# Hybrid stick-breaking / RG-LRU block: sums of output-weight blocks made in DRAM, output projection with plain loads into rotating buffers

## The chip, the core and the metric

The kernel runs on one core of a Trainium2 chip. The metric is the device time of one execution in microseconds, median of several runs. A trace of one profiled execution lists every instruction of the engines: PE (matrix multiply; PEld its weight loads), DVE (vector), ACT (scalar), POOL (GpSimd) and SP, which here only issues transfers (DMA). ACT and POOL issue transfers too, between their own instructions. All transfers run on the core's 16 DMA engines.

## The reference

```python
xn = rmsnorm(h, norm_gain[l])                       # h: (1, 512, 2048)
proj = jnp.einsum('bsd,de->bse', xn, w_in[l])       # 2048 -> 6144
q, k, v, g_sb, x_lru, g_lru = jnp.split(proj, ...)  # 1024 each
y_sb  = stick_breaking_attention(qh, kh, vh) * silu(g_sb)    # 8 heads x 128
y_lru = rg_lru(causal_depthwise_conv(x_lru)) * silu(g_lru)   # 1024 channels, 8 groups
y = jnp.concatenate([y_sb, y_lru], axis=-1)
h = h + jnp.einsum('bse,ed->bsd', y, w_out[l])      # 2048 -> 2048
```

All is float32. The kernel multiplies a float32 matrix as a high half (cast to a shorter format) and a low half (the rest), so each product takes three matmuls: high x high, high x low, low x high.

## The kernel before

**Input projection.** Four rounds p = 0 to 3, one for two heads and two LRU groups each. A round has three groups of eight chunks: `qk` (queries and keys), `xg` (LRU input and its gate), `vg` (values and attention gate). A chunk is 256 rows of w_in, loaded by SP in two transfers of 256 KB into one of four raw buffers (L214 to L221, L239), split by ACT (high, L231) and DVE (low, L232), and used in 24 matmuls. Attention weights and the LRU of a round run beside the next groups. Finished rows of y go to `y_dram`; those of the last heads and LRU groups (6, 7, 14, 15) stay in SBUF. `finish_vg` (L479) ends a round: it evacuates the values and multiplies the attention weights with them (PE L416 and L418, tile `o`).

**Output projection.** It is a Strassen-Winograd scheme: y is cut into four blocks (`a11` to `a22`, tokens by channels), w_out into 2 x 2 blocks, and seven products `p1, p7, p5, p3, p6, p2, p4` (in this order) of combinations of them give the result. Products 1, 3 and 2 use plain blocks of w_out; 7, 5, 6 and 4 use sums of blocks. A product has 2 x 4 weight tiles (m, a), each 128 x 2 x 512 (512 KB), and for each of them a pair of casts (L581 on ACT for the high half `wo`, L582 on DVE for the low half) and 12 matmuls (L627 to L629). The combinations of y (`s1`, `s3`, `s5`, `s6`, `s7`; split into `s` and `os`) are made on DVE, and so are the sums of the results with the residual x (`r`, loaded from ACT's queue, L647) before the stores (SP, L652).

**How the weight tiles come.** c1 (8 tiles) and the first half of c2 (4 tiles) are loaded by SP (L550) into slots that lie over the input projection's buffers; the second half of c2 goes into memory that attention frees (`c2_pool`, L665). A sum is made in SBUF: POOL issues a second transfer of another block onto the same tile with `accum_op=add` (L554). For c1 that happens after each split of product 1, 5 and so on (`add_to`, L659, called through `after` in `product`, L621), so c1 runs through the blocks of products 1, 5, 6, 4. c2 is loaded and added to for product 7, and reloaded (`reload`, L689) for products 3 and 2. The high and low halves rotate through two buffers `wo0`, `wo1`, and from product 7 on a third (L593).

**What sets the order.** Within an engine the instructions stand in an order that the framework's scheduler chooses from its own estimate of times; `tc.issue_after(x)` makes what follows stand behind x. At most eight transfers of SP and ACT together are under way on their eight lanes: each issue waits until the transfer that last used its lane has landed. An engine's instructions are started strictly in order, so an issue that waits holds up what stands behind it.

Of the kernel before, what the change touches and what calls it, by code (L numbers as in the profile page):

```python
# [1 line left out]

# [6 lines left out]
F32 = mybir.dt.float32  # L9
F32R = mybir.dt.float32r  # L10
# [3 lines left out]
ALU = mybir.AluOpType  # L14
# [7 lines left out]
def hybrid_block_kernel(ctx: ExitStack, tc: tile.TileContext, x, norm_gain, w_in, q_norm_gain,  # L22
                        k_norm_gain, conv_w, conv_b, lru_w_a, lru_b_a, lru_w_x, lru_b_x,
                        lru_lambda, w_out, out):
    nc = tc.nc
    P = 128
# [4 lines left out]
    KC = 2  # L31
# [3 lines left out]
    x2 = x[0]  # L35
# [178 lines left out]
    def load_w(src, name):  # L214
        t = raw_pool.tile([P, KC, 512], F32, tag="raw", name=name)
        if len(src.shape) == 4:
            for s in range(2):
                nc.sync.dma_start(t[:, :, 256 * s:256 * s + 256], src[:, :, s, :])
        else:
            nc.sync.dma_start(t, src)  # L220
        return t  # L221

# [12 lines left out]
    def in_group(a, p, vfirst, name, first=False):  # L235
# [13 lines left out]
        for c in range(NC):  # L249
# [13 lines left out]
            for b in range(4):  # L263
                for j in range(KC):
# [15 lines left out]
                    else:  # L280
# [217 lines left out]
    for p in range(4):  # L498
# [7 lines left out]
        banks = in_group(2, p, False, f"xg{p}")  # L506
# [23 lines left out]
    proj.close()  # L530
    NA = 4
# [4 lines left out]
    for tag, cols in ([(f"yl{a}", 1024) for a in (3, 2, 1, 0)] + [(f"c2_0_{a}", 1024) for a in (3, 2, 1, 0)]
                      + [("wo1", 2048), ("s3", 1024), ("s2", 1024)]
                      + [(f"c1_1_{a}", 1024) for a in (3, 2, 1, 0)]
                      + [("wo0", 2048), ("s1", 1024), ("s0", 1024)]
                      + [(f"{n}{a}", 1024) for a in (3, 2, 1, 0) for n in ("c1_0_", "ye")]):  # L540
# [23 lines left out]
    c1 = {(m, a): two(f"c1_{m}_{a}") for m in range(2) for a in range(NA)}  # L564
    c2 = {(0, a): two(f"c2_0_{a}") for a in range(NA)}
    a11, a21 = [t[:, :, 0:256] for t in ye], [t[:, :, 256:512] for t in ye]
    a12, a22 = [t[:, :, 0:256] for t in yl], [t[:, :, 256:512] for t in yl]

    for a in range(NA):
        nc.sync.dma_start(ye[a], y_dram_a[0, :, a])  # L570
        load_c(c1[0, a], 0, 0, 0, a)
    for a in range(NA):
        load_c(c1[1, a], 0, 0, 1, a)
    for a in range(NA):
        load_c(c2[0, a], 0, 1, 0, a)
        add_c(c2[0, a], 1, 1, 0, a)

    def split(t, src):
        t = t.rearrange("p (x b n) -> p x b n", x=2, b=2)
        h, l = t[:, 0], t[:, 1]  # L580
        nc.scalar.copy(h, src)  # L581
        nc.vector.tensor_tensor(out=l, in0=src, in1=h.bitcast(F32), op=ALU.subtract)  # L582
        return h, l

    def split_s(i, a, src):
# [4 lines left out]
    def split_w_out(i, m, a, src):  # L590
        n = wo_count[0] % wo_count[1]
        wo_count[0] += 1
        if n == 2:  # L593
            return split(wo_pool.tile([P, 2048], F32R, tag="wo", name=f"wo{i}_{m}{a}"), src)
        return split(held.pop(f"wo{n}") if f"wo{n}" in held else op_tile(f"wo{n}", F32R, f"wo{i}_{m}{a}"), src)
# [4 lines left out]

    finish_vg(3, banks, wts)
    for a in range(2):
# [4 lines left out]

    def product(i, banks, src, w, after=None):


        out = {}
        s = []
        for m in range(2):
            for u in range(2):
                out[m, u] = banks(m, f"p{i}_{m}{u}")
            for a in range(NA):
                if m == 0:
                    s.append(ready.pop(("s", a)) if i == 1 else split_s(i, a, src[a]))
# [39 lines left out]

    def add_to(tiles, s, h):  # L659
        return lambda m, a: add_c(tiles[m, a], s, h, m, a)  # L660

    p1 = product(1, banks_1, a11, c1, add_to(c1, 0, 1))

    mixer.close()
    c2_pool = ctx.enter_context(tc.tile_pool(name="c2", bufs=4, reuse_waits="tile"))  # L665
# [22 lines left out]

    def reload(tiles, s, h):  # L689
        return lambda m, a: load_c(tiles[m, a], s, h, m, a)  # L690

    p7 = product(7, banks_mm, s7, c2, reload(c2, 1, 1))
    for a in range(NA):
# [75 lines left out]
```

## Time and profile before

| | us |
|---|---|
| median of 3 runs | 813.45 |
| lowest, highest | 812.19, 813.66 |
| the profiled execution, its own time | 810.3 |
| its span in the trace | 808.6 |
| PE busy | 774.3 (96%) |
| DVE, ACT busy | 512.5 (63%), 441.2 (55%) |
| share of the chain that ended last: PE, DMA | 90%, 5% |

PE is busy in nearly all of the span; of the page's 40 slices the 31st to the 34th (about 606 to 687 us) show less, 7, 7, 8 and 4 tenths, where DMA stands at nine tenths or more. How to read the rows below: a row of the timeline begins with the start and the duration of what it merges (x2 means two instructions), and in brackets stands how long its engine had been idle before and what ended that. A matmul's duration includes its way through the array; the next one starts before it ends, so the time of one is read from the distance of starts.

### The profile page before, as it was taken

What the parts mean: (1) busy time and instruction counts of PE and PEld (TensorE: products, weight loads), DVE (VectorE), ACT (ScalarE), POOL (GpSimd) and SP (SyncE); (2) the same over time, 40 slices, a digit from 0 to 9 for tenths busy, and PEclk for the clock granted to TensorE, in tenths of its full rate; (3) what the DMA queues carried; (4) which work ended last, traced back from release to release, by engine and by line L of the source; (5) the groups of instructions that cost most, each with busy time, mean ns of one, the idle gap of its engine ahead of it and who ended that gap; (6) DMA issues with size and microseconds to landing.
All of it is one profiled execution on the core that took longest, in us unless ns stands there. A gap on an engine that the chain in (4) does not pass through costs nothing.

```text
span 808.6 us, 10599 instructions
## 1 busy us (share of the span) xinstructions
PE 774.3 (96%) x3847; PEld 652.3 (81%) x3847; DVE 512.5 (63%) x857; ACT 441.2 (55%) x828; POOL 42.6 (5%) x55
## 2 busy tenths in 40 slices
PE   8999999999999999999999999999997784999997
PEld 6888888888888998888899888888986562888886
DVE  4664489772547778344689753557869572776963
ACT  5844577751456867234597732456866331554451
POOL 0000000000000000000000000000001530312100
PEclk9999999999999999999999999999998886999999
DMA  9522222233232321432212342222189999999911
GB/s 294 190 79 93 90 86 79 97 118 105 79 104 60 104 95 56 143 104 88 96 60 91 96 133 91 92 80 79 52 288 283 222 262 259 198 227 179 215 53 53
DMA packets 84857, 104.55 MB, mean 129 GB/s; under 512 B 5362, under 2 KB 61252, under 8 KB 84804
## 3 DMA queue, kind: packets, MB, share of 16 engines
q1 hardware_dynamic: 73796, 82.90, 32.2%
q0 software_dynamic: 8704, 16.78, 11.8%
q10 hardware_dynamic: 2304, 4.20, 1.5%
q8 instruction: 30, 0.49, 0.3%
q14 instruction: 23, 0.19, 0.1%
HBM read 96.51 MB, written 7.34 MB: 128 GB/s over the span
## 4 chain that ended last, share of the span: by engine, by line
PE 90%; DMA 5%; issue 2%; POOL 2%; DVE 0%; SPq 0%; ACT 0%; POOLq 0%; ACTq 0%; DVEq 0%
PE p L627 5%; PE p L628 5%; PE p L629 5%; DMA c<-in_w_out_dram 4%; PE z L360 4%; PE qk0b L283 2%; PE qk0b L284 2%; PE xg0b L283 2%; PE xg3b L284 2%; PE xg1b L284 2%; PE xg2b L284 2%; PE xg0b L284 2%; PE xg1b L282 2%; PE xg2b L282 2%; PE xg3b L282 2%
## 5 line engine op out<-in xcount | busy, mean ns | idle before, releaser
L627 PE MATMUL p<-wo,os 128*128 128x512 f32 x192 | 68.9, 401 | 14.0 <-ACT wo L581 14.0
L628 PE MATMUL p<-wo,os 128*128 128x512 f32 x192 | 77.1, 402 | 1.4 <-DVE wo L582 1.4
L629 PE MATMUL p<-wo,os 128*128 128x512 f32 x192 | 76.6, 399 | 0.0
L627 PEld LDWEIGHTS p<-wo,os 128*128 128x128 f32 x192 | 36.8, 193 | 23.0 <-ACT wo L581 14.9
L628 PEld LDWEIGHTS p<-wo,os 128*128 128x128 f32 x192 | 37.1, 193 | 10.7 <-DVE wo L582 2.6
L629 PEld LDWEIGHTS p<-wo,os 128*128 128x128 f32 x192 | 37.1, 193 | 8.2
L581 ACT CAST wo<-c 128x1024 fp32r<-128x1024 f32 x12 | 12.6, 1049 | 35.2 <-DMA c<-in_w_out_dram 21.6
L582 DVE TENSOR_TENSOR wo<-c,wo 128x1024 fp32r<-128x1024 f32 x12 | 14.7, 1224 | 22.2 <-ACT wo L581 20.6
L372 ACT ACTIVATE sp<-z 128x128 f32<-128x128 f32 (+3 forms) x32 | 13.9, 435 | 25.0 <-PE z L360 24.9
L283 PE MATMUL qk0b<-xl,hqk 128*128 128x512 f32 x64 | 26.4, 413 | 0.0
L284 PE MATMUL qk0b<-xh,lqk 128*128 128x512 f32 x64 | 25.2, 394 | 0.0
L283 PE MATMUL xg0b<-xl,hxg 128*128 128x512 f32 x64 | 25.2, 394 | 0.0
L282 PE MATMUL xg1b<-xh,hxg 128*128 128x512 f32 x64 | 25.1, 393 | 0.0
L282 PE MATMUL xg3b<-xh,hxg 128*128 128x512 f32 x64 | 25.1, 393 | 0.0
L282 PE MATMUL xg2b<-xh,hxg 128*128 128x512 f32 x64 | 25.1, 393 | 0.0
L282 PE MATMUL xg0b<-xh,hxg 128*128 128x512 f32 x64 | 25.1, 392 | 0.0
L283 PE MATMUL xg3b<-xl,hxg 128*128 128x512 f32 x64 | 25.1, 392 | 0.0
L283 PE MATMUL xg1b<-xl,hxg 128*128 128x512 f32 x64 | 25.1, 392 | 0.0
L283 PE MATMUL xg2b<-xl,hxg 128*128 128x512 f32 x64 | 25.1, 392 | 0.0
L284 PE MATMUL qk1b<-xh,lqk 128*128 128x512 f32 x64 | 25.0, 390 | 0.0
L282 PE MATMUL qk2b<-xh,hqk 128*128 128x512 f32 x64 | 24.9, 389 | 0.0
L282 PE MATMUL qk3b<-xh,hqk 128*128 128x512 f32 x64 | 24.9, 389 | 0.0
(556 smaller groups left out, 2474.5 us busy)
## 6 DMA issues: line engine op xcount, KB each, us to landing
c<-in_w_out_dram SPq DMA_DIRECT2D x12, 512.0 KB, 8.5
qk0r<-in_w_in_dram SPq DMA_DIRECT2D x16, 256.0 KB, 4.9
xg0r<-in_w_in_dram SPq DMA_DIRECT2D x16, 256.0 KB, 2.9
vg0r<-in_w_in_dram SPq DMA_DIRECT2D x16, 256.0 KB, 3.1
qk1r<-in_w_in_dram SPq DMA_DIRECT2D x16, 256.0 KB, 3.0
xg1r<-in_w_in_dram SPq DMA_DIRECT2D x16, 256.0 KB, 2.8
vg1r<-in_w_in_dram SPq DMA_DIRECT2D x16, 256.0 KB, 3.0
qk2r<-in_w_in_dram SPq DMA_DIRECT2D x16, 256.0 KB, 3.1
```

Of the source, the lines that this page charges most:

```text
L282: nc.tensor.matmul(banks[b], lhsT=wh[:, cs], rhs=xh[kt], start=st, stop=False)
L283: nc.tensor.matmul(banks[b], lhsT=wh[:, cs], rhs=xl[kt], start=False, stop=False)
L284: nc.tensor.matmul(banks[b], lhsT=wl[:, cs], rhs=xh[kt], start=False, stop=sp)
L360: nc.tensor.matmul(o, lhsT=lhsT, rhs=rhs, start=start, stop=stop, skip_group_check=True)
L372: nc.scalar.activation(e, z, AF.Abs)
L581: nc.scalar.copy(h, src)
L582: nc.vector.tensor_tensor(out=l, in0=src, in1=h.bitcast(F32), op=ALU.subtract)
L627: nc.tensor.matmul(out[m, u], lhsT=sh[:, j, us], rhs=wh[:, j, :], start=st, stop=False)
L628: nc.tensor.matmul(out[m, u], lhsT=sh[:, j, us], rhs=wl[:, j, :], start=False, stop=False)
L629: nc.tensor.matmul(out[m, u], lhsT=sl[:, j, us], rhs=wh[:, j, :], start=False, stop=sp)
```

## The change

The sums of blocks that products 7, 5, 6 and 4 need are made in DRAM (`wsum`, 32 tiles of 512 KB) during the input projection. In every group except the first, behind every second chunk's load, SP copies a base block from DRAM to DRAM and POOL adds another block to it: sum 7, then 5, then 6 (base: sum 5), then 4 (base: sum 6), eight tiles each. In the output projection all tiles of w_out or wsum come by one plain load each, into 12 slots `c0` to `c11` that rotate. `wo` gets two more buffers after product 1 (four in all). The last `finish_vg` and the residual loads are placed behind the last split that was written before them.

```diff
     def in_group(a, p, vfirst, name, first=False):
...
         def load(c):
-            return load_w(w_in_v[:, KC * c:KC * c + KC, a, :, 256 * p:256 * p + 256], f"{name}r{c}")
+            t, last = load_w(w_in_v[:, KC * c:KC * c + KC, a, :, 256 * p:256 * p + 256], f"{name}r{c}")
+            if not first and c % 2 == 1 and sums:
+                with tc.issue_after(last.ins):
+                    sums.pop(0)()
+            return t
...
+    units = [(m, a) for m in range(2) for a in range(NA)]
+    wsum = {(i, m, a): dram.tile([P, 2, 512], F32, name=f"ws{i}_{m}{a}") for i in (5, 7, 6, 4) for m, a in units}
+
+    def make_sum(i, base, add, m, a):
+        nc.sync.dma_start(wsum[i, m, a], block(*base, m, a) if len(base) == 2 else wsum[base[0], m, a])
+        nc.gpsimd.dma_start(wsum[i, m, a], block(*add, m, a), accum_op=ALU.add)
+
+    sums = [partial(make_sum, i, base, add, m, a) for i, base, add in
+            ((7, (0, 1), (1, 1)), (5, (0, 0), (0, 1)), (6, (5,), (1, 1)), (4, (6,), (1, 0))) for m, a in units]
...
+    def load_c(i, m, a, src):
+        n = c_count[0] % 12
+        c_count[0] += 1
+        t = held.pop(f"c{n}") if f"c{n}" in held else op_tile(f"c{n}", F32, f"c{i}_{m}{a}")
+        t = t.rearrange("p (b n) -> p b n", b=2)
+        nc.sync.dma_start(t, src)
+        return t
...
     for a in range(NA):
         nc.sync.dma_start(ye[a], y_dram_a[0, :, a])
-        load_c(c1[0, a], 0, 0, 0, a)
-    for a in range(NA):
-        load_c(c1[1, a], 0, 0, 1, a)
-    for a in range(NA):
-        load_c(c2[0, a], 0, 1, 0, a)
-        add_c(c2[0, a], 1, 1, 0, a)
+        c1.update(load_b(1, 0, 0, [(0, a)]))
+    c1.update(load_b(1, 0, 0, units[NA:]))
+    c7 = load_sum(7, units[:NA])
...
-    finish_vg(3, banks, wts)
+    with tc.issue_after(last_hi[0].ins), tc.issue_after(last_lo[0].ins):
+        finish_vg(3, banks, wts)
...
-        nc.scalar.dma_start(t, x2[ts, ns])
+        with tc.issue_after(last_hi[0].ins):
+            nc.scalar.dma_start(t, x2[ts, ns])
...
-    for a in range(NA):
-        c2[1, a] = c2_pool.tile([P, 2, 512], F32, tag="c2", name=f"c2_1_{a}")
-        load_c(c2[1, a], 0, 1, 1, a)
-        add_c(c2[1, a], 1, 1, 1, a)
-    wo_count[1] = 3
+    wo_count[:] = [0, 4]
+    c7.update(load_sum(7, units[NA:]))
...
-    p5 = product(5, banks_o, s5, c1, add_to(c1, 1, 1))
+    p5 = product(5, banks_o, s5, c5)
+    c3 = load_b(3, 1, 1)
...
-    p3 = product(3, banks_mm, s3, c2, reload(c2, 1, 0))
+    p3 = product(3, banks_mm, s3, c3)
+    c6 = load_sum(6)
```

What this does to the order, at three places. In the names `wo7_02` is the pair of halves for product 7, m = 0, a = 2; `os7_0` the split of s7's block 0; the number at a name's end counts buffers.

PE, behind the last chunk of the last `vg` group, before:

```order
L284 MATMUL vg3b3_5654<-xh15_637,lvg3_7_1_5992 128x512
L416 MATMUL o6_6127<-wh6_5045,vh3_6099 128x512
L416 MATMUL o6_6127<-wl6_5046,vh3_6099 128x512
L416 MATMUL o7_6138<-wh7_5133,vh3_6099 128x512
L416 MATMUL o7_6138<-wl7_5134,vh3_6099 128x512
```

After the change `p1_00<-wo0` stands directly behind that last matmul of vg3; this is the end of product 1's first unit and what follows:

```order
L651 MATMUL p1_01_6248<-wo0__6152,s0__6154 128x512
L649 MATMUL p1_01_6248<-wo0__6152,s0__6154 128x512
L650 MATMUL p1_01_6248<-wo0__6152,s0__6154 128x512
L651 MATMUL p1_01_6248<-wo0__6152,s0__6154 128x512
L649 MATMUL p1_00_6247<-wo1__6145,s1__6153 128x512
L649 MATMUL p1_01_6248<-wo1__6145,s1__6153 128x512
L435 MATMUL o6_6219<-wh6_5141,vh3_6191 128x512
L435 MATMUL o6_6219<-wl6_5142,vh3_6191 128x512
L435 MATMUL o7_6230<-wh7_5229,vh3_6191 128x512
L435 MATMUL o7_6230<-wl7_5230,vh3_6191 128x512
```

The 20 matmuls of attention stood before all of product 1; now its first unit and part of its second stand before them, and the rest of attention behind the second.

DVE in the second half of product 1, after the change, from the split of its sixth unit to that of its seventh:

```order
L604 TENSOR_TENSOR wo1_11_6320<-c5__6150,wo1_11_6320 128x1024
L631 TENSOR_TENSOR yl3__6137<-o7_6230,vs7_6203 128x512
L604 TENSOR_TENSOR wo7_02_6449<-c10__6142,wo7_02_6449 128x1024
L604 TENSOR_TENSOR wo7_03_6467<-c11__6141,wo7_03_6467 128x1024
L680 TENSOR_TENSOR ye0__6162<-yl0__6140,ye0__6162 128x2x256
L710 SCALAR_TENSOR_TENSOR ye0__6162<-s7_0_6387,yl0__6140 128x2x256
L680 TENSOR_TENSOR ye3__6156<-yl3__6137,ye3__6156 128x2x256
L710 SCALAR_TENSOR_TENSOR ye3__6156<-s7_3_6393,yl3__6137 128x2x256
L680 TENSOR_TENSOR ye1__6160<-yl1__6139,ye1__6160 128x2x256
L710 SCALAR_TENSOR_TENSOR ye1__6160<-s7_1_6389,yl1__6139 128x2x256
L604 TENSOR_TENSOR wo1_12_6335<-c6__6149,wo1_12_6335 128x1024
```

Before, only two subtractions stood between the splits `wo1_11` and `wo1_12`; now nine instructions do, two of them splits for product 7 into the new buffers.

ACT, before, with residual loads between the casts of product 1:

```order
L681 COPY e1_01_6320<-p1_01_6156 128x512
L647 DMA r22_01_6657<-in_x_dram 128x512
L647 DMA r11_01_6660<-in_x_dram 128x512
L647 DMA r12_10_6663<-in_x_dram 128x512
L647 DMA r22_10_6667<-in_x_dram 128x512
L647 DMA r11_10_6670<-in_x_dram 128x512
L647 DMA r12_11_6673<-in_x_dram 128x512
L581 CAST wo1_12_6249<-c1_1_2__6053 128x1024
```

After the change all twelve first residual loads stand behind the last cast of product 5:

```order
L603 CAST wo5_12_6690<-c5_12_6556 128x1024
L603 CAST wo5_13_6705<-c5_13_6558 128x1024
L670 DMA r12_00_6736<-in_x_dram 128x512
L670 DMA r22_00_6740<-in_x_dram 128x512
L670 DMA r11_00_6743<-in_x_dram 128x512
```

They moved by about one and a half products; the casts of product 3 stand directly behind them.

## Rows read from the trace of the kernel before

**Rows 1.** Windows: start:end, length, busy (count) by engine, PEclk, DMA share, GB/s.
```profile
160.00:220.00 60.00, 60.00 (x273) 49.98 (x272) 30.70 (x50) 24.00 (x42) 0.20 (x2) 1.00 0.33 104
670.00:680.00 10.00, 0.00 (x0) 0.00 (x0) 0.00 (x0) 0.74 (x1) 0.00 (x0) 0.54 1.10 260
740.00:760.00 20.00, 20.00 (x89) 16.37 (x89) 15.84 (x21) 8.91 (x10) 7.23 (x6) 1.00 1.10 217
```

**Rows 2.** Timeline of PE: start, us, instruction, count, idle before and its releaser.
```profile
609.32 0.40 PE L284 MATMUL vg3b<-xh,lvg 128*128 128x512 f32 x1
...
643.36 1.22 PE L627 MATMUL p<-wo,s__6051 128*128 128x512 f32 x2 [5.50 <-ACT wo L581]
...
648.04 0.62 PE L627 MATMUL p<-wo,s__6050 128*128 128x512 f32 x2
...
680.36 1.22 PE L627 MATMUL p<-wo,os 128*128 128x512 f32 x2 [11.87 <-ACT wo L581]
...
798.02 0.63 PE L627 MATMUL p<-wo,os 128*128 128x512 f32 x2
...
800.76 0.62 PE L627 MATMUL p<-wo,os 128*128 128x512 f32 x2
...
803.25 0.39 PE L629 MATMUL p<-wo,os 128*128 128x512 f32 x1
```

**Rows 3.** Waits of PE, 600 to 808: total us, times, longest.
```profile
PE p L627 <- ACT wo L581: 19.5, 3, 11.9
...
PE p L628 <- DVE wo L582: 2.6, 2, 1.4
```

**Rows 4.** Timeline of ACT and its queue in the output projection.
```profile
607.73 0.63 ACT L465 ACTIVATE ql<-e0l 128x512 f32<-128x512 f32 x1
...
635.53 6.64 ACTq L647 DMA_DIRECT2D r<-in_x_dram  x4
642.26 1.04 ACT L581 CAST wo<-c__6053 128x1024 fp32r<-128x1024 f32 x1 [8.24 <-issue]
...
679.26 1.04 ACT L581 CAST wo<-c 128x1024 fp32r<-128x1024 f32 x1 [16.32 <-DMA c<-in_w_out_dram]
```

**Rows 5.** Timelines of SP's queue and of POOL: loads of c2, last addition.
```profile
604.89 0.47 SPq L550 DMA_DIRECT2D c__6045<-in_w_out_dram  x1
...
613.11 16.05 SPq L550 DMA_DIRECT2D c<-in_w_out_dram  x4
...
657.63 1.20 POOL L554 DMA_DIRECT2D c<-in_w_out_dram  x1 [3.39 <-issue]
```

**Rows 6.** DMA, 680 to 780: queues (packets, MB, share of 16 engines); issues, us to landing.
```profile
q0 software_dynamic: 4898, 9.43, 54.4%
q1 hardware_dynamic: 4704, 8.91, 31.4%
...
c<-in_w_out_dram SPq DMA_DIRECT2D x8, 512.0 KB, 4.9
...
c__6065<-in_w_out_dram POOLq DMA_DIRECT2D x2, 512.0 KB, 6.5
```

**Rows 7.** Timeline of DVE around the beginning of product 1.
```profile
605.91 0.69 DVE L461 SCALAR_TENSOR_TENSOR pl<-ql 128x512 f32<-128x512 f32 x1
...
623.51 1.21 DVE L474 TENSOR_TENSOR_SCAN hl<-e0l,e1l 128x512 f32<-128x512 f32 x1
...
628.17 1.21 DVE L582 TENSOR_TENSOR wo<-c__6059,wo 128x1024 fp32r<-128x1024 f32 x1
629.30 0.67 DVE L606 TENSOR_TENSOR yl__6041<-o,vs 128x512 f32<-128x512 f32 x1
```

**Rows 8.** Timeline of POOL in the input projection, rounds 2 and 3.
```profile
324.78 0.10 POOL L510 MEMSET xpad<- 128x3 f32 x1 [146.46 <-DVE hl L343]
...
474.07 0.10 POOL L510 MEMSET xpad<- 128x3 f32 x1 [147.14 <-DVE hl L343]
```

**Rows 9.** DMA issues of the page: issues, KB each, us to landing.
```profile
xg1r<-in_w_in_dram SPq DMA_DIRECT2D x16, 256.0 KB, 2.8
```

More of the change, by code (lines that the diff above doesn't have):

```diff
@@ L1 @@
 from contextlib import ExitStack, nullcontext
+from functools import partial
 import concourse.bass as bass
@@ L215, in load_w @@
         t = raw_pool.tile([P, KC, 512], F32, tag="raw", name=name)
[L216 to L221, printed above, removed]
+        for s in range(2):
+            last = nc.sync.dma_start(t[:, :, 256 * s:256 * s + 256], src[:, :, s, :])
+        return t, last
     def split_w(raw, j, name, first=False):
@@ L285, in in_group, with block @@
         return banks
+    NA = 4
+    w_out_a = w_out[0].rearrange("(b s a p) (h m n) -> s p a b h m n", p=P, s=2, a=NA, h=2, n=512)
+    def block(s, h, m, a):
+        return w_out_a[s, :, a, :, h, m, :]
+    units = [(m, a) for m in range(2) for a in range(NA)]
[5 more added lines that the diff above has]
+            ((7, (0, 1), (1, 1)), (5, (0, 0), (0, 1)), (6, (5,), (1, 1)), (4, (6,), (1, 0))) for m, a in units]
     qks = {}
@@ L530, in hybrid_block_kernel @@
     proj.close()
[L531 removed]
     op_pool = ctx.enter_context(tc.tile_pool(name="op", bufs=1, side="right", reuse_waits="tile"))
     slots = {}
[L536 removed]
+    for tag, cols in ([(f"yl{a}", 1024) for a in (3, 2, 1, 0)] + [(f"c{n}", 1024) for n in (11, 10, 9, 8)]
                       + [("wo1", 2048), ("s3", 1024), ("s2", 1024)]
[L538 removed]
+                      + [(f"c{n}", 1024) for n in (7, 6, 5, 4)]
                       + [("wo0", 2048), ("s1", 1024), ("s0", 1024)]
[L540 removed]
+                      + [(f"{n}{a}", 1024) for a in (3, 2, 1, 0) for n in ("c", "ye")]):
         slots[tag] = cols
@@ L563, in hybrid_block_kernel, with load_b, load_sum @@
     yl = [two(f"yl{a}") for a in range(NA)]
-    c1 = {(m, a): two(f"c1_{m}_{a}") for m in range(2) for a in range(NA)}
-    c2 = {(0, a): two(f"c2_0_{a}") for a in range(NA)}
     a11, a21 = [t[:, :, 0:256] for t in ye], [t[:, :, 256:512] for t in ye]
     a12, a22 = [t[:, :, 0:256] for t in yl], [t[:, :, 256:512] for t in yl]
+    c_count = [0]
+    def load_c(i, m, a, src):
[5 more added lines that the diff above has]
+        return t
+    def load_b(i, s, h, us=units):
+        return {(m, a): load_c(i, m, a, block(s, h, m, a)) for m, a in us}
+    def load_sum(i, us=units):
+        return {(m, a): load_c(i, m, a, wsum[i, m, a]) for m, a in us}
+    c1 = {}
     for a in range(NA):
         nc.sync.dma_start(ye[a], y_dram_a[0, :, a])
-        load_c(c1[0, a], 0, 0, 0, a)
-    for a in range(NA):
-        load_c(c1[1, a], 0, 0, 1, a)
-    for a in range(NA):
-        load_c(c2[0, a], 0, 1, 0, a)
-        add_c(c2[0, a], 1, 1, 0, a)
+        c1.update(load_b(1, 0, 0, [(0, a)]))
+    c1.update(load_b(1, 0, 0, units[NA:]))
+    c7 = load_sum(7, units[:NA])
     def split(t, src):
@@ L580, in split @@
         h, l = t[:, 0], t[:, 1]
-        nc.scalar.copy(h, src)
-        nc.vector.tensor_tensor(out=l, in0=src, in1=h.bitcast(F32), op=ALU.subtract)
+        last_hi[0] = nc.scalar.copy(h, src)
+        last_lo[0] = nc.vector.tensor_tensor(out=l, in0=src, in1=h.bitcast(F32), op=ALU.subtract)
         return h, l
+    last_hi, last_lo = [None], [None]
     def split_s(i, a, src):
@@ L592, in split_w_out @@
         wo_count[0] += 1
-        if n == 2:
-            return split(wo_pool.tile([P, 2048], F32R, tag="wo", name=f"wo{i}_{m}{a}"), src)
+        if n > 1:
+            return split(wo_pool.tile([P, 2048], F32R, tag=f"wo{n}", name=f"wo{i}_{m}{a}"), src)
         return split(held.pop(f"wo{n}") if f"wo{n}" in held else op_tile(f"wo{n}", F32R, f"wo{i}_{m}{a}"), src)
@@ L606, in hybrid_block_kernel, with product @@
         nc.vector.tensor_tensor(out=yl[k % 4][:, k // 8], in0=y, in1=gate, op=ALU.mult)
-    def product(i, banks, src, w, after=None):
+    def product(i, banks, src, w):
         out = {}
@@ L657, in tt @@
         nc.vector.tensor_tensor(out=out, in0=in0, in1=in1, op=op)
-    def add_to(tiles, s, h):
-        return lambda m, a: add_c(tiles[m, a], s, h, m, a)
-    p1 = product(1, banks_1, a11, c1, add_to(c1, 0, 1))
+    p1 = product(1, banks_1, a11, c1)
     mixer.close()
-    c2_pool = ctx.enter_context(tc.tile_pool(name="c2", bufs=4, reuse_waits="tile"))
     wo_pool = ctx.enter_context(tc.tile_pool(name="wo", bufs=1, reuse_waits="tile"))
@@ L687, in banks_o @@
         return ps_o.tile([P, 512], F32, tag="o", name=name)
-    def reload(tiles, s, h):
-        return lambda m, a: load_c(tiles[m, a], s, h, m, a)
-    p7 = product(7, banks_mm, s7, c2, reload(c2, 1, 1))
+    p7 = product(7, banks_mm, s7, c7)
+    c5 = load_sum(5)
     for a in range(NA):
@@ L714, in hybrid_block_kernel @@
         tt(r11[k], r11[k], e1[k])
-    p3 = product(3, banks_mm, s3, c2, reload(c2, 1, 0))
+    p3 = product(3, banks_mm, s3, c3)
+    c6 = load_sum(6)
     for k in MU:
         tt(r12[k], p3[k], r12[k])
-    p6 = product(6, banks_o, s6, c1, add_to(c1, 1, 0))
+    p6 = product(6, banks_o, s6, c6)
+    c2 = load_b(2, 1, 0)
     r21 = {}
@@ L731, in hybrid_block_kernel @@
     p2 = product(2, banks_mm, a12, c2)
+    c4 = load_sum(4)
     for k in MU:
@@ L734, in hybrid_block_kernel @@
         store(r11[k], 0, 0, *k)
-    p4 = product(4, banks_o, a22, c1)
+    p4 = product(4, banks_o, a22, c4)
     for k in MU:
```

8 lines of the change are left out of this document (removed).

## The prediction

> **What bounds the kernel now.** I read the windows first: up to about 600 us PE is busy in every one (60.00 of 60), with the DMA engines a third used; at 670 to 680 PE does nothing at a DMA share of 1.10; at 740 to 760 it is full again [rows 1]. So the input projection is bound by PE, and what can be won lies in the first third of the output projection. There I count in units: one unit is one (m, a) of a product, a 512 KB weight tile, two casts and 12 matmuls; 7 products x 8 units = 56, in the order p1, p7, p5, p3, p6, p2, p4; p7.4 is the fifth unit of p7, the 13th of all. A unit at full clock takes 2.74 us (800.76 - 798.02), the last matmul ends at 803.64, and the span 4.96 later [rows 2]. 56 x 2.74 = 153.4, yet from vg3's last matmul (609.7) to 803.64 there are 194. The waits of PE name the holes: 19.5 us in three waits for the high half of a weight (ACT, L581), 2.6 for the low half (DVE, L582) [rows 3]. After a hole the clock is low: the two matmuls at 643.36 take 1.22 instead of 0.63, and that unit 4.68 (to 648.04) [rows 2], so about 2.0 us lost each time. ACT's rows name the causes [rows 4]: at 642.26 it had been held 8.24 us by its own queue, where residual loads stood waiting to be issued (four of them, 6.64 us); at 679.26 it had waited 16.32 us for a block of w_out. That block, c2 for p7.4, is loaded on SP from 613.11 on (four issues over 16.05 us, since they need memory that attention frees) and then added to by POOL, whose last such issue is at 657.63 and takes 1.20 [rows 5]; under a full DMA system it lands 20 us later.
>
> **The change, part by part.** *Loads in place of load-and-add.* The 32 accumulations of this stage go; the blocks arrive by 56 plain loads where 32 loads and 32 accumulations were. From 680 to 780 the accumulations took 54.4% of the 16 engines for 9.43 MB, 3.0 us per 512 KB, the plain queue 31.4% for 8.91 MB, 1.85 us [rows 6]. A unit now asks 1.85 us in each 2.74, about two thirds; residuals and stores (32 of 256 KB, 1.2 MB per product) add some 4 us in a product's 22: DMA keeps ahead. c7's first four tiles are issued as c2's were, by 604.89 [rows 5], with no second pass. Its other four take the slots of c1's first tiles, which their splits free from about 616 on; p7.4 needs the first at 661. The 16-us waits end, and what is late next is ACT and DVE.
>
> *The new order, walked with the rows' durations.* DVE's order is the same up to the polynomial step at 605.91 (0.69) [rows 7]. Then two more dependent steps (607.3), ACT's square (0.63) [rows 4], and six DVE instructions, one held until vg3's last matmul: 611.5. ACT, in order: Ln, cast of s0, Exp, cast of wo0 (1.04): 614.2. PE formerly did the attention's 20 matmuls here; now two units stand first, so it idles from 609.7 to 614.2. The low half of wo0 waits on DVE behind s0, a product, the scan (1.21) and takes 1.21 itself: 616.4. Then ten matmuls at the low clock, 4.3: 620.7; p1.1 and attention's matmuls, 2.3 + 0.9 + 3.6: about 627.4; p1.2 and p1.3: 632.85; p1.4 a wait of 0.35, p1.5: 638.65. The next wait is the largest: between the low halves of p1.5 (done 635.35) and p1.6, DVE has a gate product, two low halves of p7 and six subtractions, 7 x 0.60 + 2 x 1.13 (steps of 629.30 - 628.17 and half that) [rows 7], then its own 1.21: 643.0. PE has started p1.6 at 638.65 with its two first matmuls and sits from 639.1 to 643.0, then runs it at low clock to 647.0. p1.7 ends at 649.8, four units of p7 with 0.4 of waiting at 661.1. p7.4 starts there instead of at 680.36: **19.3 us** earlier, with no low clock, **2.0** more. The 5.50-us hole at 643.36 goes, since the residual loads now stand behind p5's last cast.
>
> *Those loads.* Twelve issues stand on ACT between p5.7's cast and p3's first. A cast is about four units ahead of PE (a fourth wo buffer), 10.9 us. 12 x 0.35 of issue, and waiting for lanes that earlier loads hold, some 7 to 8 us, leave ACT and DVE (7 of 20 residual sums before p3.0's low half) about even with PE. I take **1.5 us** of waiting; the bounds are 0 and 8.24 us plus 2.0 of clock, the hold of before [rows 4].
>
> *The sums in DRAM.* 32 base copies on SP (between each second pair of weight loads), 32 accumulations on POOL (1.20 each to issue). From xg0 to vg2 these are eight groups of eight chunks; a round of 24 chunks takes 474.07 - 324.78 = 149.3 us [rows 8], so one sum falls into two chunks, 12.4 us. The engines are used 0.33 there [rows 1], 4.1 us, so 8.3 are free. No row shows a copy or an accumulation within DRAM. From below: 1.85 + 3.0 = 4.9 us, both as into SBUF. From above: all of the time to landing counted as engine time, 4.9 + 6.5 = 11.4 [rows 6]. I take 4.9, the same bytes through the same engines: hidden under PE. Four raw buffers give a weight load 4 x 5.5 us less 2.8 to landing [rows 9] and the split, some 17 us of slack. If the cover goes, each us above 8.3 costs 32 us, less these 17. SP's copies for sums 6 and 4 wait for an accumulation eight sums (99 us) earlier; behind them stand weight loads. POOL's memsets of xpad now stand behind sums, still some 40 us ahead of their use.
>
> The rows show w_out's blocks being read at full rate, 1.85 us per 512 KB. The Trainium skill (DMA: Bandwidth & Descriptors, Latency and other measured facts) speaks against the change here: copies between HBM tensors fell from 207 GB/s at a row pitch of 512 KiB to 103 GB/s at 4 to 8 MiB. A block's two halves lie 8 MiB apart, its rows only 8 KiB. By that page a base copy would take 2.5 to 5.1 us, an estimate; with 3.0 for the accumulation that is 8.1 at most, just hidden. It gives the third rival below a few points of its chance, and no run here shows it yet.
>
> **Sum.** -19.3 - 2.0 + 1.5 = -19.8 us. The profiled execution took 810.3 us (span 808.6): 790.5. The median of the runs is 813.45, 3.15 above it, so on that scale 793.65; I say 794.
>
> **Rivals.**
> 1. *DVE and ACT keep up better than I walked.* The hole at 639 is an order effect of some 4 us; if these few instructions run closer together, it and its low clock go: -5.9, 788. With no wait at all from 614.2 on, 614.2 + 56 x 2.74 + 3.6 + 4.96 = 776.2 in span, 781 on the median's scale. For it: the other halves of the first units miss PE's need by a few tenths only. Against: DVE's order is fixed, and nine steps stand between.
> 2. *The residual loads hold ACT as before.* They did so for 8.24 us at 642. Now twelve stand together, p3's casts directly behind. Up to 8.24 + 2.0, less the 1.5 counted, and as much of it again for the four loads before p2 as 2 us: 804. Against: four units of lead.
> 3. *Slower: the sums fill the DMA engines in the input projection.* Place: every second chunk's loads, behind a base copy on SP's ring and beside an accumulation. From 8.3 us per sum the engines are full; the slack covers up to 8.8; at 9.5 the gain is gone (32 x 1.15 = 19.8 + 17); at 10.6, midway from there to the bound, 32 x 2.3 - 17 - 19.8 = +37: 850. For it: an accumulation lands in 6.5 us even in a lighter phase. Against: the same accumulation occupied the engines for only 3.0.
> 4. *It does nothing*: the p7.4 wait is replaced by an equal one, for instance loads of ws that wait for late accumulations: 813. Against: sum 7 is made first, over 450 us before its use.
>
> **Chances.** Forecast (788 to 800) 0.66; rival 1 (781 to 788) 0.10; rival 2 (800 to 811) 0.13; rival 3 0.08; rival 4 0.03. Range 784 to 808: it leaves out the half of rival 1 below it, the upper third of rival 2, and rivals 3 and 4. About 0.2% (1.6 us) is what a measurement of this kernel can tell from no change; faster 0.89, same 0.03, slower 0.08.
>
> **What would show it.** In the windows of the changed kernel: PE full up to 609 with a DMA share of 0.6 to 0.8 up to 470 us (right), or holes of PE before 600, with weight casts released by DMA (rival 3). The first matmul of p1 near 614, before attention's last ones. No wait of a cast for a load in p7; instead a wait of about 4 us for DVE's low half in the seventh unit, near 639 to 643, with a low clock after it. p7.4 near 661. From there 44 units without a hole above 1.5 us, except between p5 and p3, where ACT's queue shows the twelve loads. The prediction is wrong if p7.4 starts after 670, if PE has holes in the projection, or if DMA is at 1.0 beyond 640.

## The result and the profile after

The changed kernel takes 793.53 us (median of 4 runs, 792.18 to 794.04) against 813.15 us for the kernel before in the same comparison (812.19 to 813.66): a ratio of 0.9757, 95% interval 0.9741 to 0.9774. Forecast was 794, in a range of 784 to 808. The profiled execution took 793.68 us, span 792.0.

The windows answer to [rows 1] (length, busy time and count of PE, PEld, DVE, ACT and POOL, granted clock, DMA share, GB/s):

```profile
160.00:220.00 60.00, 60.00 (x274) 50.08 (x273) 31.91 (x52) 24.90 (x44) 4.56 (x7) 1.00 0.83 185
670.00:680.00 10.00, 10.00 (x45) 8.20 (x44) 7.02 (x8) 5.11 (x6) 0.00 (x0) 1.00 0.84 186
740.00:760.00 20.00, 20.00 (x89) 16.30 (x88) 19.34 (x24) 9.05 (x11) 0.00 (x0) 1.00 0.70 246
```

In the input projection the DMA share went from 0.33 to 0.83 and PE is as full as it was. The window in which PE did nothing, 670 to 680, is full; the DMA share there is 0.84 where it was 1.10.

PE's timeline, for [rows 2], and its waits from 600 us on, for [rows 3]:

```profile
610.74 0.39 PE L286 MATMUL vg3b<-xh,lvg 128*128 128x512 f32 x1
...
615.27 1.22 PE L649 MATMUL p<-wo__6152,s__6154 128*128 128x512 f32 x2 [4.15 <-ACT wo__6152 L603]
...
617.51 0.80 PE L650 MATMUL p<-wo__6152,s__6154 128*128 128x512 f32 x1 [1.02 <-DVE wo__6152 L604]
...
643.85 0.80 PE L650 MATMUL p<-wo,s__6147 128*128 128x512 f32 x1 [4.05 <-DVE wo L604]
...
654.07 0.61 PE L649 MATMUL p<-wo,os 128*128 128x512 f32 x2
...
662.38 0.39 PE L649 MATMUL p<-wo,os 128*128 128x512 f32 x1
...
697.78 0.73 PE L649 MATMUL p<-wo,os 128*128 128x512 f32 x2 [2.09 <-ACT wo L603]
...
699.04 0.50 PE L650 MATMUL p<-wo,os 128*128 128x512 f32 x1 [0.53 <-DVE wo L604]
...
787.13 0.40 PE L651 MATMUL p<-wo,os 128*128 128x512 f32 x1
```
```profile
PE p L650 <- DVE wo L604: 4.6, 2, 4.1
...
PE p L649 <- ACT wo__6152 L603: 4.1, 1, 4.1
...
PE p L649 <- ACT wo L603: 2.1, 1, 2.1
...
PE p L650 <- DVE wo__6152 L604: 1.0, 1, 1.0
```

Five waits are left, 11.8 us. Those of 11.87 and 5.50 us [rows 2] are gone. The row at 654.07 begins p7.1 and that at 662.38, 36 starts later, p7.4; PE doesn't wait ahead of it. The wait at 643.85 is one for DVE, whose timeline shows what it did between the low halves of p1.5 (at 634.96) and p1.6:

```profile
636.70 1.22 DVE L604 TENSOR_TENSOR wo<-c__6142,wo 128x1024 fp32r<-128x1024 f32 x1
637.83 1.22 DVE L604 TENSOR_TENSOR wo<-c__6141,wo 128x1024 fp32r<-128x1024 f32 x1
638.97 0.69 DVE L680 TENSOR_TENSOR ye__6162<-yl__6140,ye__6162 128x512 f32<-128x512 f32 x1
...
641.98 0.68 DVE L710 SCALAR_TENSOR_TENSOR ye__6160<-s,yl__6139 128x512 f32<-128x512 f32 x1
642.58 1.22 DVE L604 TENSOR_TENSOR wo<-c__6149,wo 128x1024 fp32r<-128x1024 f32 x1
```

Two splits of p7 and six combinations of y stand ahead of the low half (642.58) that PE is waiting for. The wait at 697.78 is one for ACT, held by its own queue:

```profile
684.68 11.44 ACTq L670 DMA_DIRECT2D r<-in_x_dram  x12
696.16 0.62 ACT L603 CAST os<-s 128x512 fp32r<-128x512 f32 x1 [10.44 <-DMA r<-in_x_dram]
```

The page's DMA issues (KB each, median us to landing), beside those of [rows 6, 9]:

```profile
ws<-in_w_out_dram POOLq DMA_DIRECT2D x32, 512.0 KB, 8.3
c<-ws SPq DMA_DIRECT2D x28, 512.0 KB, 3.4
ws<-in_w_out_dram SPq DMA_DIRECT2D x16, 512.0 KB, 6.6
ws<-ws SPq DMA_DIRECT2D x16, 512.0 KB, 6.4
c<-in_w_out_dram SPq DMA_DIRECT2D x16, 512.0 KB, 5.3
...
xg1r<-in_w_in_dram SPq DMA_DIRECT2D x16, 256.0 KB, 5.9
```

A weight load now lands in 5.9 us where it took 2.8, and PE waits for none.

**Where the start scatters.** vg3's last matmul starts 1.4 us later than before (610.74 against 609.32). That is not the sums. The last high-half matmul of the very first group, qk0, starts at 58.8 us in the profile of before and at 60.2 here; over all fourteen profiles it lies between 58.8 and 62.3, and vg3's last matmul comes 550.5 us behind it in every kernel but one (the dense sums below). So below I also give the rest of the span behind vg3's last matmul, which is free of that scatter: 808.6 - 609.3 = 199.3 us before, 792.0 - 610.7 = 181.3 after.

### The profile page after: what moved, and what is told of

The parts are those of the page before. It is cut to its first block, busy times and chain, and to the rows that moved or that the text cites. A ratio compares the mean times of both kernels' runs of the same rounds, so it can differ in the third digit from the quotient of the medians.

```text
span 792.0 us, 10670 instructions
## 1 busy us (share of the span) xinstructions
PE 772.6 (98%) x3847; PEld 651.5 (82%) x3847; DVE 514.3 (65%) x857; ACT 440.8 (56%) x828; POOL 37.1 (5%) x55
## 4 chain that ended last, share of the span: by engine, by line
PE 95%; DMA 3%; DVE 1%; ACT 1%; issue 0%; SPq 0%; DVEq 0%
PE p L650 6%; PE p L651 6%; PE p L649 6%; PE z L379 4%; PE qk0b L284 2%; PE qk0b L285 2%; PE xg0b L285 2%; PE qk0b L286 2%; PE xg2b L286 2%; PE xg3b L286 2%; PE xg1b L286 2%; PE xg0b L286 2%; PE xg1b L284 2%; PE xg3b L284 2%; PE xg2b L284 2%; PE xg3b L285 2%
## 5 line engine op out<-in xcount | busy, mean ns | idle before, releaser
L603 ACT CAST wo<-c 128x1024 fp32r<-128x1024 f32 x44 | 46.0, 1048 | 36.6 <-PE p L651 34.4
L604 DVE TENSOR_TENSOR wo<-c,wo 128x1024 fp32r<-128x1024 f32 x44 | 53.5, 1222 | 19.3 <-ACT wo L603 19.3
L301 POOL DMA_DIRECT2D ws<-in_w_out_dram x32 | 33.5, 1047 | 372.4 <-DMA ws<-in_w_out_dram 180.1
L649 PEld LDWEIGHTS p<-wo,os 128*128 128x128 f32 x192 | 36.0, 188 | 10.6 <-ACT wo L603 2.5
L650 PEld LDWEIGHTS p<-wo,os 128*128 128x128 f32 x192 | 36.0, 188 | 9.6 <-DVE wo L604 1.3
L651 PEld LDWEIGHTS p<-wo,os 128*128 128x128 f32 x192 | 36.0, 188 | 8.0
```

The costliest lines, as they stand in the source:

```text
L301: nc.gpsimd.dma_start(wsum[i, m, a], block(*add, m, a), accum_op=ALU.add)
L603: last_hi[0] = nc.scalar.copy(h, src)
L604: last_lo[0] = nc.vector.tensor_tensor(out=l, in0=src, in1=h.bitcast(F32), op=ALU.subtract)
```

## The experiments

The runs were made in five groups, each with the kernel before beside it, whose median lay between 811.60 and 813.15 us. So a difference between medians of two groups can be off by some 1.5 us, and there the ratios and the rest of the span say more.

| kernel | median us (runs) | ratio to before, 95% interval | span | vg3's last matmul | rest |
|---|---|---|---|---|---|
| changed kernel | 793.53 (4) | 0.9757, 0.9741 to 0.9774 | 792.0 | 610.7 | 181.3 |
| changed, no sums made | 796.45 (4) | 0.9803, 0.9777 to 0.9829 | 797.2 | 612.3 | 184.9 |
| before, sums made unused | 811.96 (10) | 0.9998, 0.9986 to 1.0010 | 813.6 | 612.8 | 200.8 |
| changed, a sum per chunk | 804.06 (4) | 0.9883, 0.9860 to 0.9906 | 803.6 | 619.5 | 184.1 |
| changed, residual loads free | 790.58 (4) | 0.9729, 0.9712 to 0.9745 | 789.1 | 610.5 | 178.6 |
| before, residual loads moved | 818.72 (5) | 1.0063, 1.0041 to 1.0085 | 817.5 | 609.8 | 207.7 |
| changed, attention first | 793.29 (4) | 0.9755, 0.9732 to 0.9779 | 790.7 | 611.8 | 178.9 |
| changed, two split buffers | 802.05 (4) | 0.9867, 0.9844 to 0.9891 | 801.9 | 611.2 | 190.7 |
| changed, combinations later | 788.36 (4) | 0.9707, 0.9684 to 0.9730 | 786.8 | 609.7 | 177.1 |
| changed, residuals on POOL | 790.51 (4) | 0.9732, 0.9704 to 0.9760 | 788.6 | 610.3 | 178.3 |
| both edits | 784.41 (4) | 0.9662, 0.9636 to 0.9688 | 782.9 | 610.6 | 172.3 |
| both, first splits earlier | 779.43 (4) | 0.9600, 0.9576 to 0.9624 | 777.3 | 610.0 | 167.3 |
| the same, two split buffers | 789.38 (5) | 0.9715, 0.9701 to 0.9728 | 787.5 | 610.6 | 176.9 |

### Are the sums hidden?

The changed kernel without them:

```
+    plain = {5: (0, 0), 7: (0, 1), 6: (1, 1), 4: (1, 0)}
+    sums = []
     def load_sum(i, us=units):
-        return {(m, a): load_c(i, m, a, wsum[i, m, a]) for m, a in us}
+        return load_b(i, *plain[i], us)
```

> Leaves out: no sum is made in DRAM; products 5, 7, 6 and 4 take a plain block of the output weights in place of the sum, from the same number of loads of the same size. Theory H (the 32 sums are wholly hidden under the projection): 793.5 us, within 0.8 us of the changed kernel, with the DMA share of the projection back from about 0.77 to about 0.3 and the last matmul of vg3 where it was. Rival C (the sums slow the projection or its start a little, as the last vg3 matmul at 610.74 us instead of 609.32 us would have it): 792 us, the last vg3 matmul back at 609.3.

796.45 us, slower than with the sums, which neither theory had. The projection is as long as ever (550.5 us from qk0 to vg3), so the sums cost it nothing. The rest is 3.6 us longer. Its loads all come from w_out itself, where 28 of 44 came from packed sums:

```profile
c<-in_w_out_dram SPq DMA_DIRECT2D x44, 512.0 KB, 5.3
```
```profile
740.00:760.00 20.00, 20.00 (x89) 16.29 (x88) 16.40 (x23) 9.45 (x11) 0.00 (x0) 1.00 0.96 263
```
```profile
701.71 0.74 PE L651 MATMUL p<-wo,os 128*128 128x512 f32 x2 [2.94 <-ACT wo L605]
702.97 0.50 PE L652 MATMUL p<-wo,os 128*128 128x512 f32 x1 [0.52 <-DVE wo L606]
```

A load of a packed sum lands in 3.4 us, one of a block in 5.3; the DMA share at 740 to 760 is 0.96 instead of 0.70. The wait ahead of product 3, where ACT's issues stand behind other transfers, grew from 2.09 to 2.94 us, and this time the clock fell after it (0.78 from 705 to 710 us). So the sums in DRAM also make the later loads cheaper. That is not the whole of the 3.6 us: 1.5 of them lie in product 1 (37.6 us instead of 36.1), whose loads are the same in both kernels; 0.85 are the longer wait, and product 3 behind it takes 1.4 more. This profile is also that of the slowest of the four runs.

The kernel before, with the sums made in the same way and never read:

> The kernel before, with the 32 sums made in DRAM during the projection as the changed kernel makes them, and never read. H: 813.2 us, as before, within 0.8 us. C: 814.6 us or more. Should the sums' writes disturb what follows the projection, 816 us or more.

811.96 us, a ratio of 0.9998: they cost nothing that can be measured. (The profile, that of the slowest of the ten runs, has a rest 1.5 us longer than before; the median shows nothing of it.)

The changed kernel with twice the density:

```
-            if not first and c % 2 == 1 and sums:
+            if not first and sums:
```

> The changed kernel with a sum behind every chunk of the projection instead of every second one, so all 32 in about 200 us. In the changed kernel the DMA engines are busy 0.77 of 12.4 us per sum, 9.5 us, of which 3.6 us were there before (0.29), so a sum takes 5.9 us of them. Theory D (the engines can't be busy over 1.0, and the projection waits for what is over): a chunk of 6.2 us now asks for 1.8 + 5.9 = 7.7 us, 1.5 us too much, 32 times, 48 us less what the buffered chunks hold back, some 15 us: 825 us (810 to 845), PE with holes between 60 and 270 us. Rival Q (the weight loads get their share first and the sums fall behind, still done long before product 7): 793.5 us, no holes, the DMA share near 1.0 for some 250 us.

804.06 us: between the theories. The profile has one hole in the projection, at the low half of a weight for qk1, and a low clock behind it (windows, and the page's landings):

```profile
PE qk1b L286 <- DVE lqk L230: 6.6, 1, 6.6
```
```profile
190.00:195.00 5.00, 0.13 (x1) 0.13 (x1) 1.47 (x3) 0.00 (x0) 1.03 (x1) 0.53 0.93 203
195.00:200.00 5.00, 5.00 (x12) 3.93 (x13) 1.62 (x3) 0.00 (x0) 0.63 (x1) 0.50 0.95 162
```
```profile
ws<-in_w_out_dram SPq DMA_DIRECT2D x16, 512.0 KB, 13.6
...
qk1r<-in_w_in_dram SPq DMA_DIRECT2D x16, 256.0 KB, 13.8
```

From qk0 to vg3 it took 560.1 us, 9.6 more. The engines were full (DMA share 1.01 to 1.03 from 60 to 220 us), and weight loads landed in 13.8 us instead of 5.7. But the hole is not a weight that came late: DVE, which makes the low half, had itself stood still until 193.53:

```profile
193.53 0.69 DVE L362 TENSOR_TENSOR y<-o,vs 128x512 f32<-128x512 f32 x1 [15.40 <-DMA y_dram<-y]
```

It waited for the buffer of a store of y, which SP had issued at 176.81 behind a sum's copy and which landed only then; in the changed kernel the same instruction waited 4.05 us. PE has no other wait in the projection, and the sums ended near 260 us. My estimate, 48 us less some 15 that buffered chunks hold back, took every over-used microsecond for a loss of PE.

### The residual loads

The changed kernel with these loads free to be issued when their buffers are:

```
-        with tc.issue_after(last_hi[0].ins):
-            nc.scalar.dma_start(t, x2[ts, ns])
+        nc.scalar.dma_start(t, x2[ts, ns])
```

> The changed kernel with the residual loads free to be issued as early as their buffers are, as before. They stand then between product 1's last splits and product 7's first on ACT's queue, 12 issues of about 0.95 us. Theory M (moving them is worth the 8.24 us idle of ACT that the kernel before shows, less the 2.6 us hole ahead of product 3): 797 to 801 us. Rival N (with DVE as product 1's bound, the ACT queue has 7 us to spare there, so moving them was worth nothing): 791 to 794.5 us, with the hole ahead of product 3 gone and one of about 2 us ahead of product 7's first unit.

790.58 us: theory N, though 0.4 below its range and without the hole that it expected ahead of product 7's first unit. The wait ahead of product 3 is gone. The loads now hold ACT in product 1, where in the changed kernel it waited 7.58 us for PE anyhow (first that kernel, then this one):

```profile
648.53 1.05 ACT L603 CAST wo<-c__6144 128x1024 fp32r<-128x1024 f32 x1 [7.58 <-PE p L651]
```
```profile
641.84 6.82 ACTq L669 DMA_DIRECT2D r<-in_x_dram  x6
648.77 1.05 ACT L603 CAST wo<-c__6144 128x1024 fp32r<-128x1024 f32 x1 [7.56 <-DMA r<-in_x_dram]
```

The same move alone, in the kernel before (`issue_after` added there):

> The kernel before with one part of the change alone: the residual loads are issued behind product 5's last split. Theory N (in the kernel before, ACT's issues held product 1's split a=2 at m=0, the 5.50 us hole at 643.36; but the bases and the accumulations are late behind it anyway, so product 7 doesn't start earlier): 812 to 814 us, the hole at 643 gone, that at p7.4 longer by as much. Theory M (the hole and its low clock come off the end): 806 us, 5.5 + 2.0 less. With the residual loads no longer among the transfers of 640 to 680 us, p7.4's accumulations may land up to 16 x 256 KB / 263 GB/s = 16 us x 0.5 earlier, 8 us: 800 us at the least.

818.72 us, slower than before: both theories missed. The 5.50-us hole at 643.36 [rows 2] did go, and p7.4 started 8.5 us earlier, at 671.88. But then the twelve issues held ACT behind product 5:

```profile
671.88 1.22 PE L629 MATMUL p<-wo,os 128*128 128x512 f32 x2 [11.81 <-ACT wo L581]
...
714.70 1.22 PE L629 MATMUL p<-wo,os 128*128 128x512 f32 x2 [6.26 <-ACT wo L581]
```
```profile
700.23 12.80 ACTq L650 DMA_DIRECT2D r<-in_x_dram  x12
713.08 0.62 ACT L581 CAST os<-s 128x512 fp32r<-128x512 f32 x1 [11.80 <-DMA r<-in_x_dram]
```

with waits of 6.26 and 1.19 us at the beginning of product 3 and 3.08 in product 2's first unit. This part of the change is a loss in either kernel. The wait for the accumulation at p7.4 stayed (11.81 us); it is gone only where the blocks come by plain loads.

Issued by POOL (`nc.gpsimd.dma_start`, no rule on when):

> The changed kernel with the 16 residual loads issued by POOL, which has nothing to do in the output projection, instead of ACT, and with no rule on when. Theory N (each of the 12 issues holds the issuing engine for about 0.95 us and nothing else about them costs time): as with the loads left free on ACT's queue, 790.6 us (789.5 to 791.8), no hole ahead of product 3, product 7's first split on ACT where it was in the changed kernel. Rival: it isn't the issues but the 4 MB of transfers among the loads of blocks: 793 us or more, with a wait for a block's load in product 7 or 5.

790.51 us, as foreseen: what cost was ACT's time for the issues behind product 5, not the transfers.

### The order and the depth

Attention's last part first again (the `with` around `finish_vg(3, ...)` taken out):

> The changed kernel with the attention's last part ahead of product 1, as before (its matmuls, and its instructions on ACT and DVE). PE then has the attention's 20 matmuls, 4.6 us, to do before product 1, but each waits for ACT or DVE. Theory P (putting product 1 first is worth about what the prediction took, the start at 614 us in place of about 620 us less the 4.6 us that return later): 795 to 798 us, PE idle ahead of product 1 for 6 us or more in all. Rival: the start is bound by the same splits either way: 793.5 us, within 1.

793.29 us: the rival. Product 1 starts 5.5 us behind vg3's last matmul (617.28 us) instead of 4.5, and waits 2.06 us at 629.58, but the later holes are smaller (1.42 us at 643.77 instead of 4.05, 1.56 ahead of product 3): what the new order gave at the start it gave back. In the profile the rest is even 2.4 us shorter than in the changed kernel.

Two buffers of split weights (`wo_count[:] = [0, 2]`):

> The changed kernel with two buffers of split weights in place of four from product 7 on. A buffer then comes free when PE ends unit n, and ACT (1.05 us) and DVE (1.23 us, and 0.69 us for a sum of y or an add to a bank) must fill it within unit n+1, 2.74 us. Theory: 48 units with 0.1 to 0.5 us lost in each and more where DVE has other work: 803 us (798 to 815). Rival: hidden: 793.5 us.

802.05 us, in the range, but not as described. From 660 to 680 PE is full; the loss stands where ACT or DVE has a burst of other work: 6.68 us ahead of product 3, and low halves 0.97 and 0.64 late at 709.86 and 740.72, and 1.41, 1.71 and 1.13 between 750 and 760 us.

```profile
700.32 1.22 PE L649 MATMUL p<-wo,os 128*128 128x512 f32 x2 [6.68 <-ACT wo L603]
```

The kernel before had three buffers from product 7 on. No run has three in the changed kernel, so the share of the fourth in its gain is not shown.

The six combinations and product 7's first splits behind product 1's last split:

```
+    lows = []
...
+                with tc.issue_after(lows[7].ins) if i == 7 else nullcontext():
-                wh, wl = ready.pop(("w", m, a)) if ("w", m, a) in ready else split_w_out(i, m, a, w[m, a])
+                    wh, wl = ready.pop(("w", m, a)) if ("w", m, a) in ready else split_w_out(i, m, a, w[m, a])
+                lows.append(last_lo[0])
...
+        with tc.issue_after(lows[(12, 12, 13, 14)[a]].ins):
-        tt(a21[a], a22[a], a21[a], ALU.subtract)
+            tt(a21[a], a22[a], a21[a], ALU.subtract)
...
```

> The changed kernel with the six combinations of y and product 7's first splits kept behind product 1's last split on DVE (the combinations behind product 7's fifth to seventh splits). Theory V (these eight instructions are the 4.05 us wait for the low half at 643.85 us, and that hole is what makes the clock low afterwards): 793.5 - 4.1 - 2 = 787.5 us (786.5 to 789.5), no hole over 0.5 us between 618 and 690 us, the clock 1.00 from 640 to 680. Rival W (the wait moves on to product 7's first splits, whose combinations of y come from DVE too): 790 to 793 us, with a hole at p7.0 to p7.3 in its place.

788.36 us: theory V. The wait at 643.85 is 0.32 us, the clock stays at 1.00 from 640 to 680, and product 7's splits did not become late:

```profile
638.85 0.50 PE L654 MATMUL p<-wo,s__6147 128*128 128x512 f32 x1 [0.32 <-DVE wo L604]
```

The rest is 4.2 us shorter, less than the 5.2 of the medians: behind the wait ahead of product 3, here 2.41 us, the clock fell this time (0.66 from 691 to 696 us).

Both edits:

> The changed kernel with both edits: the residual loads issued by POOL, and the combinations of y and product 7's first splits behind product 1's last split on DVE. Theory (the two holes are independent): 788.4 - 2.9 = 785.5 us (784.5 to 786.8), PE without a hole over 1 us from 618 us to the end. Rival (one covers the other): 788 us.

784.41 us, 0.1 us below the theory's range: the two gains add up (5.2 and 3.0 us alone, 9.1 together). What was left was the start of product 1, for which a cast stood on ACT behind the recurrence of the last LRU group:

```
+        gate = silu_gate(gbank, n)
+        def tail():
-        nc.vector.tensor_scalar(out=q, in0=q, scalar1=-1.0, scalar2=1.0, op0=ALU.mult, op1=ALU.add)
+            nc.vector.tensor_scalar(out=q, in0=q, scalar1=-1.0, scalar2=1.0, op0=ALU.mult, op1=ALU.add)
...
-        gated(8 + g, y, silu_gate(gbank, n))
+            gated(8 + g, y, gate)
+        if g == 7:
+            return tail
+        tail()
...
         ready["w", 0, a] = split_w_out(1, 0, a, c1[0, a])
+        if a == 0:
+            with tc.issue_after(last_hi[0].ins), tc.issue_after(last_lo[0].ins):
+                tail()
```

> The kernel with both edits, and the recurrence's last part of head group 7 (from its square's complement on) behind product 1's first splits instead of ahead of them on ACT and DVE. Theory (product 1's first matmul waits 4.15 us for a cast that itself stands behind a 3.13 us wait of ACT for the recurrence on DVE): the first matmul of product 1 about 1.5 us behind the projection's last instead of 4.5, 785.5 - 3 = 782.5 us, less up to 1.5 more where the clock then doesn't fall (781 to 784). Rival (the splits' buffers or the loads of y and the blocks come only then): 785.5 us, the cast still at 612 us or later.

779.43 us, more than foreseen, and 14.1 us below the changed kernel. ACT casts the first half as soon as it has the square, and product 1 follows the projection without a gap (PE, then ACT):

```profile
610.01 0.39 PE L286 MATMUL vg3b<-xh,lvg 128*128 128x512 f32 x1
610.27 0.73 PE L663 MATMUL p<-wo__6143,s__6145 128*128 128x512 f32 x2
611.95 0.50 PE L664 MATMUL p<-wo__6143,s__6145 128*128 128x512 f32 x1 [0.94 <-DVE wo__6143 L611]
```
```profile
608.66 0.60 ACT L610 CAST s__6145<-ye__6153 128x512 fp32r<-128x512 f32 x1
609.17 1.05 ACT L610 CAST wo__6143<-c__6152 128x1024 fp32r<-128x1024 f32 x1
```

In the changed kernel these casts began at 613.15 and 614.19 us. The granted clock is 1.00 over the whole span. The rest of 167.3 us is 5.0 below that of both edits, and about half of that each are waits and clock: PE's waits behind vg3 come to 2.8 us instead of 5.4 (4.1 are gone, but 1.14 and 0.61 are new), and product 1 begins at a granted clock of 1.00 (610 to 615 us) instead of 0.51 (615 to 620).

With two buffers of split weights in that kernel:

> The kernel with all three edits (779.43 us), with two buffers of split weights in place of four. With four and two buffers the changed kernel took 793.53 and 802.05 us, and nearly all that difference stood at two places: ahead of product 3, where ACT issues twelve residual loads (PE idle 6.68 in place of 2.09 us), and around 740 to 760 us, where it issues four more. Theory (the depth is worth something only where ACT is held): 779.4 us, within 1.5. Rival (two buffers cost some tenths in each unit where DVE also has sums to make): 784 us or more, with PE idle ahead of low halves in products 7, 5 and 6.

789.38 us: the rival, and my reading of the first two-buffer run was too narrow. ACT no longer issues loads, yet PE waits 7.0 us, six times, for DVE:

```profile
PE p L664 <- DVE wo L611: 7.0, 6, 1.9
```

With four buffers it was 1.7 us, twice. Between the low halves that it begins at 734.16 and 739.50 us DVE has six sums for the output and a low half of y, 0.6 us each; four buffers carry PE over such bursts, two don't. Behind two of the waits, 1.85 us at 655.72 and 1.84 at 740.77, the clock was low as well:

```profile
655.72 0.50 PE L664 MATMUL p<-wo,os 128*128 128x512 f32 x1 [1.85 <-DVE wo L611]
```

## Why the prediction was right, and where it was not

**The removed wait** was right in place and size. p7.4 was walked to 661.1 us for a projection that ended where it did in [rows 2]; with the start 1.4 us later that is 662.5, and the profile has 662.38. The walk to it holds too, within 0.9 us at every unit: first matmul 614.2 + 1.4 = 615.6 (615.27 measured), first low half 617.8 (617.51), the wait in the seventh unit until 644.4 (643.85; 4.05 us, 3.9 foreseen), by the instructions named. Moving those took the wait away, for 4.2 us of the rest and 5.2 of the medians.

**The cause given for the 5.50-us hole was right, the credit for the move was wrong.** "The 5.50-us hole at 643.36 goes, since the residual loads now stand behind p5's last cast": it would have gone anyway. With the loads free, they hold ACT for 7.56 us in a stretch in which it waits for PE anyhow. The move cost 2.95 us by the medians (793.53 - 790.58), where 1.5 was taken, against nothing gained; rival 2 was thus real in kind, small in size.

**The term for these loads was too small.** 1.5 us of waiting was taken, 2.09 + 0.53 = 2.62 measured, and 3.4 in all: with the loads on POOL p7.4 also starts at 662.38, and the last matmul at 783.73 instead of 787.13. ACT was held 10.4 us, near the 11 to 12 reckoned. The clock did not fall after it in this profile, as it did in the one without sums.

**The unit** of 2.74 us, read from one pair, is nearly right for the kernel before: from the third matmul of product 3 to the last there are 381 starts, 716.01 to 803.25, 0.2290 us each, 2.75 a unit. After the change the same starts take from 699.04 to 787.13, 0.2312 each, 2.77 a unit. The sum silently takes the 44 units from p7.4 on to be as long after the change as before. With the loads on POOL, so without a wait, they take 121.35 us to the last start; before it was 122.89, of which about 2.2 are p7.4 at the low clock (4.93 us instead of 2.75). So they became slower by some 0.6 us; why is not shown.

**The sums in DRAM** were sized too small, within their bounds, and without consequence. The DMA queues from 60 to 480 us (packets, MB, share of 16 engines), first before, then after:

```profile
q1 hardware_dynamic: 39904, 39.07, 29.1%
```
```profile
q1 hardware_dynamic: 43850, 54.45, 40.8%
q0 software_dynamic: 8395, 16.18, 31.5%
```

16.18 MB are 30.9 accumulations in 0.315 x 420 us: 4.3 us of the engines each, where 3.0 was taken from those into SBUF. The copies add 15.4 MB, 29.3 of them, for 0.117 x 420 us: 1.7 each (1.85 taken), if all that this queue has more is put down to them. Together 6.0, not 4.9, and below the 8.3 that were free. Rival 3's price was too high besides: at 6.2 us to a sum instead of 12.4 the loss was 9.6 us, and it came by a path that the prediction did not name, a store of y that DVE waited for, with no weight late.

The Trainium skill (DMA: Bandwidth & Descriptors, Latency and other measured facts) has copies within HBM fall to half at row pitches of 4 to 8 MiB. Here the copies from w_out (rows 8 KiB apart, halves 8 MiB apart) land in 6.6 us and those between packed sums in 6.4: the rule's slowdown does not appear in this layout, whose rows lie closer than any of the page's.

**The agreement is closer than the sum was.** Profile against profile the change is 810.3 - 793.68 = 16.6 us, not 19.8. The 3.2 us between are the start (1.4), the residual loads (3.4 - 1.5 = 1.9) and the slower units (0.6), less 0.5 at the end (792.0 - 787.5 = 4.5 instead of 4.96), 0.2 of clock and 0.1 of the walk. That forecast and median still lie within 0.5 us is luck: 3.15 us were added because the profile of before lay that far below its own median, while that of after is at its median, and this made up for the 3.2; 1.4 us of it is the scatter of the start.

## What to carry to other kernels

Where a stage waits for load-and-add transfers and an earlier stage leaves the DMA engines two thirds idle, making the sums there can be free: it cost nothing at a DMA share of 0.83 and 9.6 us at 1.02, where a store that another engine waited for landed late. Packed results load faster too. Before a step is moved, look whether the engine that it holds is waiting anyway: the same twelve issues were free in product 1, cost 3 us behind product 5, and cost nothing on an engine without other work. After the large wait is gone, read in the bound engines' own order what stands ahead of the instruction that PE waits for; three such places were worth another 14 us, 0.9600 of the time before against 0.9757. And once the loads are in time, the depth of the split buffers decides who rides over bursts: two in place of four cost 8.5 us here, and 10 in the fastest kernel.

## What the runs showed of the hardware that was not expected

- Loading 512 KB takes 3.4 us to land from a packed tensor and 5.3 from blocks of two rows of 2 KB per partition.
- An accumulation into DRAM keeps the DMA engines busy for 4.3 us per 512 KB and lands in 8.3; into SBUF it was 3.0 and 6.5 [rows 6].
- A wait of 2.09 and 0.53 us left the granted clock at 1.00 (697 to 705 us), one of 2.94 and 0.52 was followed by 0.78 and one of 2.41 and 0.53 by 0.66; but one of 1.85 alone was followed by 0.53 (656 to 659 us, two buffers in the fastest kernel), so the length of a wait does not tell by itself. In the profile with no wait over 1.14 us the clock stayed at 1.00 for the whole span.
- With the DMA engines at 1.02 a store of 256 KB, issued at 176.81 us, kept an engine waiting until 193.53; such stores landed in 2.1 us in the median.
- The first group of the program ends anywhere within 3.5 us, in kernels whose beginning is the same, and the 550.5 us behind it are equal in all but one. Each kernel has one profile, so how much of the difference between runs of one kernel this is has not been shown.
